# Attention masks on VectorE instead of TensorE, and forgetting rows as a full 128-row matmul

## The chip, the cores and the metric

The kernel runs on one core of one Trainium2 chip. The metric is the device time of one execution in microseconds (us). Before the change the median of three runs is 1434.82 us (1432.43 to 1436.96). The engines are named as in the profile: PE (TensorE, matmuls; PEld its weight loads), DVE (VectorE), ACT (ScalarE), POOL (GpSimd) and SP (SyncE, which issues most of the loads).

## The reference, cut to what matters

256 tokens of 1024 features go through four layers. Three of them have softmax attention that the change touches: layer 0 (16 heads of forgetting attention and 16 of dilated attention) and the two mixers of the second block (8 heads each, with two attentions per head over the same queries).

```python
def forgetting_attention(q, k, v, log_f):
    c = jnp.cumsum(log_f, axis=1).transpose(0, 2, 1)
    ...
        s = jnp.einsum('bqhd,bkhd->bhqk', q[:, q0:e], k[:, :e]).astype(f32) * scale
        s = s + c[:, :, q0:e, None] - c[:, :, None, :e]
        causal = jnp.arange(e)[None, :] <= (q0 + jnp.arange(BLOCK))[:, None]
        p = jax.nn.softmax(jnp.where(causal, s, NEG), axis=-1)

def dilated_pattern(q, k, v, window, dilation):
    ...
    s = jnp.where(mask, s, NEG)
    lse = jax.nn.logsumexp(s, axis=-1)
    p = jnp.exp(s - lse[..., None])
```

The three dilated patterns are merged with weights from their log-denominators. On 256 tokens that equals one softmax over scores to which the logarithm of the number of patterns that hold a key is added, and the kernel computes it so: its dilated mask holds such logarithms, and -1e30 where no pattern holds the key.

## The kernel before

Every product with weights is computed as three matmuls (`mm3`, L177 to L179) on operands that are split into a high and a low part. ScalarE writes the high half of a loaded weight tile (L56), VectorE the low one (L58); this goes on through the whole kernel, a few tiles ahead of use. The weights are used in units; a unit of 128x256 matmuls has 48 of them in two chunks.

Attention runs beside the units, as side work in stages (class `Side`). One attention step treats two heads and both query tiles of 128 tokens. Stage 1 computes the scores on PE: S1 (second query tile, 256 keys for each of two heads, 512 columns; L419) and S0 (first tile, 128 keys, 256 columns; L422), three matmuls each, and adds the mask by more matmuls into the same bank. Stage 2 (`softmax`) runs on VectorE and ScalarE. Stage 3 transposes the probabilities on PE (L456, L458), stage 4 multiplies them with the values (L468, L470). Between the stages stand chunks of weight matmuls: in layer 0 a stage follows after two chunks, in the mixers after one. So what a stage needs from the other engines has the time of one or two chunks to come about.

How a mask gets into the scores before:
- dilated steps (8, first half of layer 0): the identity times the mask, in two parts, four matmuls (`dil`, L557 with 512 columns and L559 with 256)
- forgetting steps (8, second half of layer 0): a matmul of two rows deep, ones times the high and the low part of the accumulated gates (`fox`, L569 and L571), and then the causal mask as identity times mask, 256 columns (`causal`, L429), once for S1 and once for S0
- mixer steps (8 in each of two mixers): the two causal matmuls alone

`softmax` then takes the maxima of S1 and S0 from PSUM on VectorE (L435, L436), ScalarE computes four exponentials from PSUM with these as bias (L441), VectorE the reciprocals (L443; in the mixers times gates, L446) and the scaling of P1 (L448), ScalarE the scaling of P0 (L449).

The tile framework orders the instructions of each engine when the program is built; each engine then works through its own queue in that order, and waits by semaphores.

Of the kernel before, what the change touches and what calls it, by code (L numbers as in the profile page):

```python
# [24 lines left out]
class Weights:  # L25
    """The weights in the order of their use: loaded and split into two float32r parts ahead of it."""
# [48 lines left out]
class Side:  # L75
    """Work in stages that goes between the weight units. A stage that yields "pre" has its next one before a unit."""
# [39 lines left out]
class Stack:  # L116
# [41 lines left out]
    def split_shifts(self):  # L158
        """The shifts of the norms, [(part, chunk), 128 features] in three bfloat16 parts that add up to them."""
# [21 lines left out]
    def evac(self):  # L181
        """What is left to do with the products of the units before; some of it a unit later."""
# [8 lines left out]
    def feature_unit(self, done, chunks=2):  # L191
        """[features, tokens] of a unit's columns."""
# [10 lines left out]
    def token_units(self, *dones):  # L203
        """[tokens, features] of the columns of some units, tile by tile of the tokens."""
# [15 lines left out]
    def finish(self, ahead=True):  # L220
        """The norm of the second tile of tokens."""
# [59 lines left out]
    def rsqrt(self, mul, eps, *var):  # L281
        """1 / sqrt(var * mul + eps) of each, by Newton's steps from a guess on the bits; the guess is negative."""
# [27 lines left out]
    def squares(self, tt, acc):  # L310
        """The sums of the squares of a tile of x, by halves of the features; acc has its banks for the squares."""
# [5 lines left out]
    def rms(self, g, accs, between=0):  # L317
        """xT gets the parts of the normalised tiles of x; g has the scales of the features."""
# [13 lines left out]
    def layer_norm(self, tt, g, b, bT=None, acc=None, rms=None):  # L332
        """Of ALPHA * x + acc; or of the normalised x by the scales in rms, with their norm's factor in this one's."""
# [41 lines left out]
    def transpose(self, tt, src, dr, shift=None, scale=None):  # L375
        """The two parts of src * r * scale + shift go to xT; dr has the scales r of the tokens on its diagonal."""
# [25 lines left out]
    def split_into(self, hi, lo, src, scale=1.0):  # L402
        """The two float32r parts of src * scale; scale is a power of two."""
# [12 lines left out]
    def scores(self, q, kz, extra):  # L416
        S1, S0 = self.bank([128, 2, 256]), self.bank([128, 2, 128])
        for i, (a, b) in enumerate(((0, 0), (0, 1), (1, 0))):
            self.nc.tensor.matmul(S1[:], q[a][:, 128:256], kz[b][:], start=i == 0, stop=False, skip_group_check=True)  # L419
        extra(S1, S0, 1)  # L420
        for i, (a, b) in enumerate(((0, 0), (0, 1), (1, 0))):
            self.nc.tensor.matmul(S0[:], q[a][:, 0:128], kz[b][:, :, 0:128], start=i == 0, stop=False,  # L422
                                  skip_group_check=True)
        extra(S1, S0, 0)
        return S1, S0

    def causal(self, S1, S0, i):
        m = self.cm[:, None, :].to_broadcast([128, 2, 128])
        self.nc.tensor.matmul((S1[:, :, 128:256] if i else S0[:]), self.identr[:], m, start=False, stop=True,  # L429
                              skip_group_check=True)  # L430
# [1002 lines left out]
```

## Time and profile before

| what | value |
|---|---|
| median of three runs | 1434.82 us |
| span of the profiled execution | 1432.7 us |
| PE busy | 1393.4 us (97%), 10075 matmuls |
| PEld busy | 1289.3 us (90%) |
| DVE busy | 1097.8 us (77%), 1816 instructions |
| ACT busy | 828.4 us (58%), 1388 instructions |
| POOL busy | 99.5 us (7%) |
| mean granted TensorE clock | 0.989 |

A busy share is a mean over stages that have different limits. Matmuls overlap: one is listed with 0.28 us where the next starts 0.12 us later, so for PE the distance of the starts tells the cost, and not the duration. The rows below are taken from single stretches for that reason. Layer 0's attention steps lie between 42 and 270 us, the mixers' between 552 and 622 and between 880 and 950 us.

### The profile page before, as it was taken

Reading aid. Unit: us, or ns where it says so; the run is one execution under the profiler, and the core shown is the slowest. Engines: PE = TensorE matmul, PEld = TensorE weight load, DVE = VectorE, ACT = ScalarE, POOL = GpSimd, SP = SyncE. Lnnn points to the kernel's source line nnn. Section 1 sums busy time; section 2 is a strip of 40 time slices with the busy share of each in tenths; the row PEclk is TensorE's granted clock in tenths of the full one; section 3 lists DMA queues with packets and bytes.
Section 4 is the critical chain, followed back from the end, with each engine's and each line's share of the span. In section 5 each row is a group of like instructions: output and inputs, shape, how many; then the busy total and the mean of one; then the engine's idle time right before and its main releaser. Section 6 shows DMA issues by size and latency. Waiting matters only on the chain. (4 is left out here: it accounts for less than half of the span.)

```text
span 1432.7 us, 25068 instructions
## 1 busy us (share of the span) xinstructions
PE 1393.4 (97%) x10075; PEld 1289.3 (90%) x10075; DVE 1097.8 (77%) x1816; ACT 828.4 (58%) x1388; POOL 99.5 (7%) x136
## 2 busy tenths in 40 slices
PE   7999999999999999999999999998999999999995
PEld 7999999789999789989999889987999999999983
DVE  7766656567777679878655388777989989989987
ACT  7665555454455347544444247645777777777762
POOL 1000000000000100010000000003010110120110
PEclk9999999999999999999999999998999999999997
DMA  7633343336444466326455446322989889889882
GB/s 292 233 147 138 129 148 138 134 138 226 155 175 155 132 232 224 118 67 264 178 184 199 176 145 253 118 98 83 361 332 339 314 327 346 307 335 355 309 329 85
DMA packets 45435, 301.50 MB, mean 210 GB/s; under 512 B 6000, under 2 KB 6368, under 8 KB 10624
## 3 DMA queue, kind: packets, MB, share of 16 engines
q1 hardware_dynamic: 42336, 293.40, 55.4%
q0 software_dynamic: 2832, 6.42, 1.7%
q8 instruction: 81, 1.33, 0.4%
q14 instruction: 42, 0.34, 0.1%
q10 hardware_dynamic: 144, 0.01, 0.0%
HBM read 298.73 MB, written 1.05 MB: 209 GB/s over the span
## 5 line engine op out<-in xcount | busy, mean ns | idle before, releaser
L58 DVE TENSOR_TENSOR w_lo<-w_raw,w_hi 128x1024 fp32r<-128x1024 f32 x553 | 673.5, 1249 | 170.0 <-ACT w_hi L56 169.7
L56 ACT ACTIVATE w_hi<-w_raw 128x1024 fp32r<-128x1024 f32 x553 | 560.9, 1056 | 212.2 <-PE ps L179 103.4
L177 PE MATMUL ps<-xT,w_hi 128*128 128x256 f32 x1096 | 310.6, 283 | 0.0
L178 PE MATMUL ps<-xT,w_hi 128*128 128x256 f32 x1096 | 308.0, 281 | 0.0
L179 PE MATMUL ps<-xT,w_lo 128*128 128x256 f32 x1096 | 307.8, 281 | 0.0
L177 PEld LDWEIGHTS ps<-xT,w_hi 128*128 128x128 f32 x1096 | 206.4, 188 | 1.7 <-issue 1.5
L178 PEld LDWEIGHTS ps<-xT,w_hi 128*128 128x128 f32 x1096 | 206.6, 188 | 0.0
L179 PEld LDWEIGHTS ps<-xT,w_lo 128*128 128x128 f32 x1096 | 206.5, 188 | 0.0
L178 PE MATMUL ps<-w_lo,xe 128*128 128x256 f32 x704 | 199.3, 283 | 1.3 <-DVE w_lo L58 1.1
L177 PE MATMUL ps<-w_hi,xe 128*128 128x256 f32 x704 | 198.9, 283 | 0.0
L179 PE MATMUL ps<-w_hi,xe 128*128 128x256 f32 x704 | 198.8, 282 | 0.0
L177 PE MATMUL ps<-w_hi,xT 128*128 128x256 f32 x528 | 148.7, 282 | 0.0
L178 PE MATMUL ps<-w_lo,xT 128*128 128x256 f32 x528 | 147.8, 280 | 0.0
L179 PE MATMUL ps<-w_hi,xT 128*128 128x256 f32 x528 | 146.9, 280 | 0.1
L178 PEld LDWEIGHTS ps<-w_lo,xe 128*128 128x128 f32 x704 | 132.5, 188 | 3.0 <-DVE w_lo L58 2.2
L177 PEld LDWEIGHTS ps<-w_hi,xe 128*128 128x128 f32 x704 | 132.9, 189 | 0.6
L179 PEld LDWEIGHTS ps<-w_hi,xe 128*128 128x128 f32 x704 | 132.6, 188 | 0.0
L177 PEld LDWEIGHTS ps<-w_hi,xT 128*128 128x128 f32 x528 | 100.0, 189 | 0.3
L178 PEld LDWEIGHTS ps<-w_lo,xT 128*128 128x128 f32 x528 | 100.0, 189 | 0.3
L179 PEld LDWEIGHTS ps<-w_hi,xT 128*128 128x128 f32 x528 | 99.2, 189 | 0.4 <-DVE xT L398 0.3
L441 ACT ACTIVATE P<-ps,sm_mx 128x128 f32<-128x128 f32 (+1 forms) x128 | 52.1, 419 | 37.3 <-DVE sm_mx L435 37.3
L1214 POOL TENSOR_TENSOR x<-x,part 128x512 f32<-128x512 f32 x28 | 47.5, 1724 | 337.2 <-ACT part L1210 274.8
(365 smaller groups left out, 2219.9 us busy)
## 6 DMA issues: line engine op xcount, KB each, us to landing
w_raw<-in_wts SPq DMA_DIRECT2D x271, 1024.0 KB, 4.9
w_raw<-in_wth SPq DMA_DIRECT2D x11, 512.0 KB, 4.5
w_raw<-in_ln_g POOLq DMA_DIRECT2D x3, 512.0 KB, 4.2
w_raw<-in_ln_b POOLq DMA_DIRECT2D x3, 512.0 KB, 5.1
x<-in_x SPq DMA_DIRECT2D x4, 256.0 KB, 3.5
out<-x SPq DMA_DIRECT2D x4, 256.0 KB, 2.1
dec<-in_dec POOLq DMA_DIRECT2D x1, 512.0 KB, 9.7
w_raw<-in_final_norm POOLq DMA_DIRECT2D x1, 512.0 KB, 3.8
```

Source lines behind the costliest of these rows:

```text
L56: self.nc.scalar.activation(hi[:, d], t[:, d], AF.Copy)
L58: self.nc.vector.tensor_sub(lo[:, d], t[:, d], hi[:, d].bitcast(F32))
L177: t.matmul(out, l[0], r[0], start=start, stop=False, skip_group_check=True)
L178: t.matmul(out, l[0], r[1], start=False, stop=False, skip_group_check=True)
L179: t.matmul(out, l[1], r[0], start=False, stop=stop, skip_group_check=True)
L441: s.activation(p[:, h, :], src[:, h, :], AF.Exp, bias=mx[:, o + h:o + h + 1], accum_out=rs[:, o + h:o + h + 1])
L1214: nc.gpsimd.tensor_add(x, x, t[:])
```

## The change

PE no longer adds masks. `scores` has three score matmuls per bank, and a fourth in the forgetting steps, for the accumulated gates; that one now has 128 rows, all ones on one side, and on the other two rows of gates and 126 of zeros (two fixed buffers `crs`, cleared once at the start, of which the loads write the first two rows). In `softmax` a combined VectorE operation takes each head's scores from PSUM, adds the mask from SBUF, multiplies by -1, writes the result to the tile of the probabilities and reduces it to its minimum; the exponentials read that tile and write over it. The masks are loaded as plain float32 tiles through GpSimd's queue (before: one load through SyncE's), and four VectorE copies, one ScalarE copy and the split of the dilated mask at the start are gone. Docstrings and comments are gone too, so the line numbers differ.

```diff
-    def scores(self, q, kz, extra):
+    def scores(self, q, kz, row=None):
         S1, S0 = self.bank([128, 2, 256]), self.bank([128, 2, 128])
-        for i, (a, b) in enumerate(((0, 0), (0, 1), (1, 0))):
-            self.nc.tensor.matmul(S1[:], q[a][:, 128:256], kz[b][:], start=i == 0, stop=False, skip_group_check=True)
-        extra(S1, S0, 1)
...
+        for S_, t, n in ((S1, 1, 256), (S0, 0, 128)):
+            ms = [(q[a][:, t * 128:(t + 1) * 128], kz[b][:, :, 0:n]) for a, b in ((0, 0), (0, 1), (1, 0))]
+            if row is not None:
+                ms.append((self.ones[:], row[:, :, 0:n]))
+            for i, (l, r) in enumerate(ms):
+                self.nc.tensor.matmul(S_[:], l, r, start=i == 0, stop=i == len(ms) - 1, skip_group_check=True)
...
-        v.reduce_max(mx[:, 0:2], S1[:], axis=AX, negate=True)
-        v.reduce_max(mx[:, 2:4], S0[:], axis=AX, negate=True)
...
-        for p, src, o in ((P1, S1, 0), (P0, S0, 2)):
+        both = ((P1, S1, mask, 0), (P0, S0, mask[:, 128:256], 2))
+        for p, src, m, o in both:
             for h in range(2):
-                s.activation(p[:, h, :], src[:, h, :], AF.Exp, bias=mx[:, o + h:o + h + 1],
+                v.tensor_tensor_reduce(p[:, h, :], src[:, h, :], m, -1.0, 3e38, ALU.add, ALU.min,
+                                       mx[:, o + h:o + h + 1])
+        for p, src, m, o in both:
+            for h in range(2):
+                s.activation(p[:, h, :], p[:, h, :], AF.Exp, bias=mx[:, o + h:o + h + 1], scale=-1.0,
                              accum_out=rs[:, o + h:o + h + 1])
...
-        nc.sync.dma_start(dm[:], a["dm"])
+        self.causal = c.tile([128, 256], F32, name="causal")
+        nc.gpsimd.dma_start(self.causal[:], a["dm"][:, 256:512])
...
-            ones = big.tile([2, 128], F32R, name="ones2")
-            dm = [big.tile([128, 256], F32R, name=f"dm{i}") for i in range(2)]
+            self.ones = big.tile([128, 128], F32R, name="ones")
+            crs = [big.tile([128, 2, S], F32R, name=f"cr{i}") for i in range(2)]
+            nc.gpsimd.memset(self.ones[:].bitcast(F32), 1.0)
+            for t in crs:
+                nc.gpsimd.memset(t[:].bitcast(F32), 0.0)
...
+            dilated = big.tile([128, 256], F32, name="dilated")
+            nc.gpsimd.dma_start(dilated[:], a["dm"][:, 0:256])
...
-                    nc.vector.tensor_copy(self.identr[:], self.ident)
-                    nc.vector.tensor_copy(self.cm[:], dmf[:, 256:384])
-                    nc.vector.tensor_scalar(ones[:], self.ident[0:2, :], 0.0, 1.0, op0=ALU.mult, op1=ALU.add)
-                    self.split_into(dm[0][:], dm[1][:], dmf[:, 0:256])
                     self.split_shifts()
...
-                cr = io.tile([2, 2, S], F32R, name="cr")
+                cr = crs[p % 2]
                 for j in range(2):
                     nc.gpsimd.dma_start(cr[j:j + 1], cc[j][2 * p:2 * p + 2, :])
```

The order of the instructions on an engine, as the programs are built, at two places. First PE's queue in the first forgetting step before (`ps` are the scores, `kz` the keys, `q` the queries, `cr` the gates, `cm` the causal mask, `w_hi` the next unit's weights):

```order
L419 MATMUL ps<-kz_86,q_1853 128x512
L419 MATMUL ps<-kz_87,q_1853 128x512
L419 MATMUL ps<-kz_86,q_1854 128x512
L569 MATMUL ps<-cr,ones_81 128x512
L429 MATMUL ps<-cm,identr 128x2x128
L422 MATMUL ps<-kz_86,q_1853 128x256
L422 MATMUL ps<-kz_87,q_1853 128x256
L422 MATMUL ps<-kz_86,q_1854 128x256
L571 MATMUL ps<-cr,ones_81 128x256
L429 MATMUL ps<-cm,identr 128x256
L177 MATMUL ps<-w_hi,xT_126 128x256
```

And the same step's rows on PE in the changed kernel, where all score matmuls stand on one line:

```order
L424 MATMUL ps<-kz_89,q_1835 128x512
L424 MATMUL ps<-kz_90,q_1835 128x512
L424 MATMUL ps<-kz_89,q_1836 128x512
L424 MATMUL ps<-cr_82,ones 128x512
L424 MATMUL ps<-kz_89,q_1835 128x256
L424 MATMUL ps<-kz_90,q_1835 128x256
L424 MATMUL ps<-kz_89,q_1836 128x256
L424 MATMUL ps<-cr_82,ones 128x256
L177 MATMUL ps<-w_hi,xT_129 128x256
```

The two causal matmuls are gone, and the gates' matmul closes each bank. Second, VectorE's queue in the first mixer, from the hidden layer of the compression (`hid`) over the first step's softmax to its scaling of P1, before:

```order
L885 TENSOR_TENSOR hid_5666<-ps,b_5652 32x256
L435 TENSOR_REDUCE sm_mx<-ps 128x2
L436 TENSOR_REDUCE sm_mx<-ps 128x2
L58 TENSOR_TENSOR w_lo<-w_raw,w_hi 128x1024 x2
L443 RECIPROCAL sm_rs<-sm_rs 128x4
L58 TENSOR_TENSOR w_lo<-w_raw,w_hi 128x1024
L446 TENSOR_TENSOR sm_rs<-sm_rs,gt 128x2 x2
L58 TENSOR_TENSOR w_lo<-w_raw,w_hi 128x1024
L448 TENSOR_SCALAR P_6174<-P_6174,sm_rs 128x256 x2
```

And VectorE at the same place in the changed kernel, down to the same reciprocal:

```order
L867 TENSOR_TENSOR hid_5640<-ps,b_5626 32x256
L436 ISA P_6144,sm_mx<-ps,causal 128x256
L436 ISA sm_mx 128x1
L436 ISA P_6144,sm_mx<-ps,causal 128x256
L436 ISA sm_mx 128x1
L436 ISA P_6145,sm_mx<-ps,causal 128x128
L436 ISA sm_mx 128x1
L436 ISA P_6145,sm_mx<-ps,causal 128x128
L436 ISA sm_mx 128x1
L58 TENSOR_TENSOR w_lo<-w_raw,w_hi 128x1024 x2
L442 RECIPROCAL sm_rs<-sm_rs 128x4
```

Eight instructions stand where two stood; what follows them is in the same order as before.

## Rows read from the trace of the kernel before

**Rows 1.** Busy us (instructions) of PE, PEld, DVE, ACT, POOL; PE clock, DMA share, GB/s.

```profile
42.00:270.00 228.00, 227.47 (x1747) 208.69 (x1747) 145.69 (x241) 134.02 (x310) 8.03 (x16) 1.00 0.41 149
551.00:569.00 18.00, 16.94 (x135) 15.72 (x134) 17.61 (x32) 12.85 (x31) 0.00 (x0) 1.00 0.72 267
```

**Rows 2.** PE by time, first forgetting step: start us, us, engine, line, tiles.

```profile
160.71 0.86 PE L419 MATMUL ps<-kz,q 128*128 128x512 f32 x3
161.51 0.49 PE L569 MATMUL ps<-cr,ones 2*128 2x512 f32 x1
161.93 0.39 PE L429 MATMUL ps<-cm,identr 128*128 128x256 f32 x1
162.15 0.52 PE L422 MATMUL ps<-kz,q 128*128 128x256 f32 x3
162.60 0.38 PE L571 MATMUL ps<-cr,ones 2*128 2x256 f32 x1
162.91 0.39 PE L429 MATMUL ps<-cm,identr 128*128 128x256 f32 x1
163.13 0.28 PE L177 MATMUL ps<-w_hi,xT 128*128 128x256 f32 x1
```

**Rows 3.** PE by time, mask matmuls of a dilated step.

```profile
102.60 0.63 PE L557 MATMUL ps<-dm,identr 128*128 128x512 f32 x2
103.06 0.52 PE L422 MATMUL ps<-kz,q 128*128 128x256 f32 x3
```

**Rows 4.** PE by time, a causal matmul of a mixer step.

```profile
570.19 0.28 PE L429 MATMUL ps<-cm,identr 128*128 128x256 f32 x1
570.30 0.52 PE L422 MATMUL ps<-kzs,q 128*128 128x256 f32 x3
```

**Rows 5.** PE by time, a 24-row matmul behind a 512-column one.

```profile
623.76 0.40 PE L179 MATMUL ps<-w_hi,yc 128*128 128x512 f32 x1
624.09 0.60 PE L382 MATMUL ps<-chunk,shifts 24*128 24x512 bf16 x2
```

**Rows 6.** VectorE's groups by form: count, busy us, mean ns, idle before.

```profile
L435 DVE TENSOR_REDUCE sm_mx<-ps 128x2 f32<-128x512 f32 x32 | 21.8, 681 | 3.2 <-PE ps L429 2.0
L436 DVE TENSOR_REDUCE sm_mx<-ps 128x2 f32<-128x256 f32 x32 | 13.4, 418 | 1.4 <-PE ps L429 1.1
L611 DVE SCALAR_TENSOR_TENSOR y<-o,g 128x256 f32<-128x256 f32 x16 | 6.6, 413 | 0.4 <-PE o L470 0.4
L1164 DVE SCALAR_TENSOR_TENSOR he<-th,ps 128x128 f32<-128x128 f32 x8 | 2.3, 282 | 0.1
L446 DVE TENSOR_TENSOR sm_rs<-sm_rs,gt 128x2 f32<-128x2 f32 x32 | 3.6, 154 | 0.3
```

**Rows 7.** By time: scalings of probabilities, and transposes on PE that follow them.

```profile
50.58 0.41 PE L458 MATMUL ps<-cst,P 128*128 128x128 f32 x2 [0.48 <-DVE P L448]
...
559.41 0.62 PE L456 MATMUL ps<-cst,P 128*128 128x128 f32 x2 [0.69 <-ACT P L449]
560.40 0.41 PE L458 MATMUL ps<-cst,P 128*128 128x128 f32 x2 [0.37 <-DVE P L448]
...
568.22 0.69 ACT L449 ACTIVATE P<-P,sm_rs 128x128 f32<-128x128 f32 x2 [2.19 <-DVE sm_rs L446]
568.84 0.27 PE L456 MATMUL ps<-cst,P 128*128 128x128 f32 x1
...
575.06 0.62 DVE L448 TENSOR_SCALAR P<-P,sm_rs 128x256 f32<-128x256 f32 x2
575.81 0.27 PE L456 MATMUL ps<-cst,P 128*128 128x128 f32 x1
```

**Rows 8.** By time, a dilated step: last scaling, and first transpose.

```profile
106.02 0.70 ACT L449 ACTIVATE P<-P,sm_rs 128x128 f32<-128x128 f32 x2 [0.25 <-DVE sm_rs L443]
109.28 0.27 PE L456 MATMUL ps<-cst,P 128*128 128x128 f32 x1
```

**Rows 9.** ScalarE by time: its first split of a weight.

```profile
10.24 2.00 ACT L56 ACTIVATE w_hi<-w_raw 128x1024 fp32r<-128x1024 f32 x2 [2.89 <-DMA w_raw<-in_wts]
```

More of the change, by code (lines that the diff above doesn't have):

```diff
@@ L427, in causal @@
[L427 to L430, printed above, removed]
-    def softmax(self, P, S1, S0, gate=None):
+        for S_, t, n in ((S1, 1, 256), (S0, 0, 128)):
[4 more added lines that the diff above has]
+                self.nc.tensor.matmul(S_[:], l, r, start=i == 0, stop=i == len(ms) - 1, skip_group_check=True)
@@ L433, in softmax @@
+        return S1, S0
+    def softmax(self, P, S1, S0, mask, gate=None):
         v, s = self.nc.vector, self.nc.scalar
         mx, rs = self.small(4, "sm_mx"), self.small(4, "sm_rs")
-        v.reduce_max(mx[:, 0:2], S1[:], axis=AX, negate=True)
-        v.reduce_max(mx[:, 2:4], S0[:], axis=AX, negate=True)
         P1 = P.tile([128, 2, 256], F32, name="P1")
         P0 = P.tile([128, 2, 128], F32, name="P0")
-        for p, src, o in ((P1, S1, 0), (P0, S0, 2)):
+        both = ((P1, S1, mask, 0), (P0, S0, mask[:, 128:256], 2))
+        for p, src, m, o in both:
@@ L492, in setup @@
         self.pick = cst[:, 200:210]
-        self.identr, self.cm = (c.tile([128, 128], F32R, name=n) for n in ("identr", "cm"))
         self.xT = [c.tile([128, 8, S], F32R, name=f"xT{i}") for i in range(2)]
@@ L519, in even, with shifts @@
             P = ctx.enter_context(tc.tile_pool(name="l0p", bufs=2))
-            dmf = io.tile([128, 384], F32, name="v")
-            self.setup(dmf)
-            def masks():
+            dilated = big.tile([128, 256], F32, name="dilated")
+            nc.gpsimd.dma_start(dilated[:], a["dm"][:, 0:256])
+            self.setup()
+            def shifts():
                 yield
@@ L526, in masks @@
                 with self.W.behind(self.W.after), self.W.behind(self.W.after_act):
-                    nc.vector.tensor_copy(self.identr[:], self.ident)
-                    nc.vector.tensor_copy(self.cm[:], dmf[:, 256:384])
-                    nc.vector.tensor_scalar(ones[:], self.ident[0:2, :], 0.0, 1.0, op0=ALU.mult, op1=ALU.add)
-                    self.split_into(dm[0][:], dm[1][:], dmf[:, 0:256])
                     self.split_shifts()
-            self.pend.append(masks())
+            self.pend.append(shifts())
             def fa_done(ps):
@@ L551, in fa_done @@
                 self.split_into(cc[0][:], cc[1][:], z)
-            def dil(S1, S0, i):
-                for j in range(2):
-                    m = dm[j][:, None, :].to_broadcast([128, 2, 256])
-                    if i:
-                        nc.tensor.matmul(S1[:], self.identr[:], m, start=False, stop=j == 1, skip_group_check=True)
-                    else:
-                        nc.tensor.matmul(S0[:], self.identr[:], m[:, :, 128:256], start=False, stop=j == 1,
-                                         skip_group_check=True)
             def fox(p):
-                cr = io.tile([2, 2, S], F32R, name="cr")
+                cr = crs[p % 2]
                 for j in range(2):
                     nc.gpsimd.dma_start(cr[j:j + 1], cc[j][2 * p:2 * p + 2, :])
-                def f(S1, S0, i):
-                    if i:
-                        nc.tensor.matmul(S1[:], ones[:], cr[:], start=False, stop=False, skip_group_check=True)
-                    else:
-                        nc.tensor.matmul(S0[:], ones[:], cr[:, :, 0:128], start=False, stop=False,
-                                         skip_group_check=True)
-                    self.causal(S1, S0, i)
-                return f
+                return cr
             pairs, vs, gs = {}, {}, {}
@@ L600, in attend @@
                 q, kz = pairs.pop(i)
-                S1, S0 = self.scores(q, kz, fox(i) if ch < 8 else dil)
+                S1, S0 = self.scores(q, kz, fox(i) if ch < 8 else None)
                 yield "pre"
-                P1, P0 = self.softmax(P, S1, S0)
+                P1, P0 = self.softmax(P, S1, S0, self.causal if ch < 8 else dilated)
                 yield
@@ L799, in attend @@
                 gate = [gt[:, tt, c0:c0 + 8].rearrange("p (g h) -> p g h", g=2)[:, :, p] for tt in range(2)]
-                S1, S0 = self.scores([t[:, p, :] for t in q], kz[kind], self.causal)
+                S1, S0 = self.scores([t[:, p, :] for t in q], kz[kind])
                 yield "pre"
-                P1, P0 = self.softmax(P, S1, S0, gate)
+                P1, P0 = self.softmax(P, S1, S0, self.causal, gate)
                 yield
@@ L1363, in constants @@
     n = sum(((d >= 0) & (d <= wd) & (d % r == 0)).astype(np.int64) for wd, r in ((128, 1), (512, 4), (2048, 16)))
-    c["dm"] = np.concatenate([np.where(n > 0, np.log(np.maximum(n, 1)), NEG), np.where(s <= t, 0.0, NEG)],
+    c["dm"] = np.concatenate([np.where(n > 0, np.log(np.maximum(n, 1)), NEG), np.zeros((128, 128)),
+                              np.where(s <= t, 0.0, NEG)],
                              axis=1).astype(np.float32)
```

6 lines of the change are left out of this document (1 added, 5 removed).

## The prediction

> **What bounds the kernel now.** I read the busy time by stretch first, then the PE instructions in order of time around the three kinds of attention step, then VectorE's groups by form, then what stands beside the few waits of PE. In the stretch that holds the first layer's sixteen attention steps PE is busy 227.47 of 228.00 us at full granted clock while VectorE is busy 145.69 and ScalarE 134.02 [rows 1]. There the matmul stream is the bound: an instruction taken out of it takes its step (the time from its start to the next one's start) out of the run, as long as nothing that PE later needs comes later than PE gets to it. The exception is a stretch at the head of each mixer: between 551 and 569 us VectorE is busy 17.61 of 18.00 us and PE only 16.94 [rows 1]. There VectorE is the bound, and whatever is added to it is paid. The change takes from PE and gives to VectorE, so these two stretches decide.
>
> **PE, forgetting steps (8).** In [rows 2] three 512-column score matmuls start at 160.71; the matmul with the forgetting rows (L569, 2 rows deep) starts 0.80 later, the next one 0.42 after that, and the unit's next weight matmul (L177) comes at 163.13. The step takes 2.42 us. A 512-column matmul on 128 rows has a step of 0.23 us (two in 0.46) [rows 3], a 256-column one 0.11 to 0.12 [rows 4]; I use 0.23 and 0.115. With these alone the ten matmuls would take 4 x 0.23 + 6 x 0.115 = 1.61 us, so about 0.8 us of each step is the price of going in and out of the 2-row form twice: L419 to L569 0.80 instead of 0.69, L569 to L429 0.42 instead of 0.23, L429 to L422 0.22 instead of 0.115, and again around L571. A 24-row matmul elsewhere shows the way in too: 0.33 us from a 512-column matmul to L382 [rows 5] where 0.23 is the step between equals. After the change the step has four 512- and four 256-column matmuls, all on 128 rows: 1.38 us. Saved: 2.42 - 1.38 = 1.04 us, times 8 = 8.3 us; 1.8 of it are the two causal matmuls, 6.5 the 2-row form.
>
> The Trainium skill, page "TensorE: Matmul & The Clock Gate", section "LDWEIGHTS (loading the stationary operand)", says that the load time depends on the columns and not on the contraction rows, so that a 32x128 load costs what a 128x128 load does. By it full rows save nothing, and only the two causal matmuls would count. The load alone is not what the rows above show as the price, so I go by them, and keep the other outcome as the first rival.
>
> **PE, dilated steps (8) and mixer steps (16).** A dilated step drops two 512- and two 256-column mask matmuls: 2 x 0.23 + 2 x 0.115 = 0.69 us, times 8 = 5.5. A mixer step drops two 256-column ones: 0.23 us, times 16 = 3.7. Sum taken out of PE: 8.3 + 5.5 + 3.7 = 17.5 us.
>
> **VectorE and ScalarE.** A softmax had two maxima, 681 and 418 ns [rows 6]. It now has four operations that read scores from PSUM and a mask from SBUF and write the masked scores, each followed by a one-column instruction that brings out the minimum. The nearest rows for the wide ones are L611 (PSUM and SBUF in, SBUF out, 256 columns, 413 ns) and L1164 (128 columns, 282 ns); for the narrow one L446 (154 ns) [rows 6]. Full price: 2 x 413 + 2 x 282 + 4 x 154 = 2006 ns against 1099, so +0.9 us. Low end: the narrow ones hide, and neighbours overlap, as two operations of L448 take 0.62 us together [rows 7]; then +0.13. I take x = 0.6 us a softmax, above the middle since each narrow one must wait for the wide one in front of it. ScalarE's four exponentials stay, now from SBUF and in place; the first may start after one 256-column operation instead of after the 512-column maximum, so on an idle VectorE the chain to the probabilities is about as long as before.
>
> **Where x is covered.** In the first layer the probabilities lie ready long before PE transposes them: the last scaling ends at 106.02 + 0.70 = 106.72 and the transposes start at 109.28 [rows 8], 2.6 us of slack; the other steps but one have 2.0 to 4.0. If that cover were gone, each step would cost x. The exception is the first step, where PE already waits 0.48 us for VectorE (the row at 50.58) [rows 7]. There the chain hangs on VectorE's queue and not on the scores, so the 0.69 us that PE saves ahead of it is lost, and some of x: I take 1.0 us. First layer: 8.3 + 5.5 - 1.0 = 12.8 us.
>
> **Where x is paid.** In each mixer PE waits for the probabilities of the first step (0.69 us for ScalarE, then 0.37 more for VectorE), takes up the second step's as they are made (its scaling runs 568.22 to 568.91, PE starts at 568.84) and the third's with 0.13 us to spare (575.68 and 575.81) [rows 7]. Behind the maxima in VectorE's queue stand the low halves of the weights (L58) and then the scalings that PE waits for, so each of these three is later by x, and PE's own saving ahead of it (0.23, 0.23, some 0.14) is only waited away: 3x + 0.6 us a mixer. The other five have more spare or an idle VectorE ahead of them. Both mixers, since the second repeats the first: 3.7 - 2 x (3 x 0.6 + 0.6) = -1.1 us, a small loss; with x = 0.13 it is +1.7, with 0.9 it is -2.9.
>
> **The start.** The 192 KB of masks leave SyncE's queue, where they stood behind the first weight, and 256 KB go by GpSimd's queue, behind its memsets, of which there are three more, and ahead of the six small loads of norm shifts, needed only after some 23 us. ScalarE waits 2.89 us for the first weight [rows 9]; 256 KB at the 267 GB/s of [rows 1] is 1.0 us if all of it cuts in ahead of that weight, and 0 if it lands behind. I take 0.2. The first mask is not read before some 45 us, and the four VectorE copies that disappear save nothing in a stretch where PE streams. GpSimd's loads of the forgetting rows keep their two buffers.
>
> **Sum.** 12.8 - 1.1 - 0.2 = 11.5 us. The profiled span is 1432.7 us; the median of the runs shown is 1434.8, 2.1 us above it, which I leave as it is: 1434.8 - 11.5 = 1423.3 us. Ends: 12.8 + 1.7 = 14.5 us saved (1420.3) and 12.8 - 2.9 - 1.0 = 8.9 (1425.9).
>
> **The rivals.** First, the depth of the forgetting matmul is not what costs, but, say, the matmuls' own place in the group: then 6.5 us stay and the time is 1423.3 + 6.5 = 1429.8. The rule of the Trainium skill named above would give this outcome. For it: the 2-row weight load itself is no different. Against it: every 2-row and 24-row neighbour in [rows 2] and [rows 5] shows the longer step. Second, PE's saving comes through whole, because VectorE's queue is put together so that nothing ahead of the scalings is later: 1434.8 - 17.5 = 1417.3. For it: at the end of a stage VectorE has idle time. Against it: the 17.61 of 18.00. Third, slower: the new wide operation is of a kind that no row of this trace shows (the built program has it as an instruction of its own class), and it may run well below one column a cycle. The price is paid in the mixers' first three steps, 6x in all, and from x = 2 also in the first layer, whose shortest slack that is. The saving is gone when 6x = 12.6 + 3.7 - 1.2 = 15.1, at x = 2.5; with x = 3.0 the mixers lose 15.5 and, with slacks of 2.0 to 2.6 overrun in four steps, the first layer about 2, which gives 1434.8 - 12.6 + 15.5 + 2 = 1439.7. Against it: VectorE's other two-input rows lie within 20 ns of each other whatever they compute. That the change doesn't do what it says is excluded: the order above has the mask matmuls gone from PE.
>
> **How the numbers follow.** Forecast, with its ends 1420.3 to 1425.9: 0.77. PE's saving whole, 1417.3: 0.08. The depth costs nothing, 1429.8: 0.06. The new operation slow: 0.09, of it 0.05 slower and 0.04 within what can be told apart. A measurement of this kernel can tell about 0.3% (4.3 us) from no change, so the line is at 1430.5. Faster: 0.77 + 0.08 + 0.03 (half of the first rival, which stands almost on the line) = 0.88; same 0.03 + 0.04 = 0.07; slower 0.05. The range reaches from the whole saving to the first rival: 1417 to 1429.
>
> **What would show it.** Right: a forgetting step of 1.4 us from its first score matmul to the next unit's L177, a dilated one without its 0.69; PE busy some 17 us less in all; softmaxes with 1.6 to 1.8 us of VectorE time; PE's waits for the transposed probabilities grown from 1 us to about 3 in each mixer. Wrong: a step of 0.42 still standing behind the matmul with the forgetting rows; wide operations over 0.6 us; PE idle ahead of transposes in the first layer's later steps; a first weight that lands later than 10.2 us.

## The result, and the profile after

The changed kernel takes 1419.52 us (median of four runs, 1418.13 to 1420.65) against 1435.29 us for the kernel before on the same chip (1432.43 to 1436.96): a ratio of 0.9889, 95% interval 0.9877 to 0.9901. It is faster by 15.8 us, where 11.5 were forecast. The profiled execution has a span of 1417.2 us, against 1432.7 before.

To see where the time went, I took each weight matmul (L177 to L179; both programs have 8652 of them, in the same order) and subtracted its start before from its start after. The changes of that difference, stretch by stretch:

| stretch (times of before) | what it holds | difference, us |
|---|---|---|
| 0 to 42 | start | +0.2 |
| 42 to 101 | first four dilated steps | -3.4 |
| 101 to 160 | last four dilated steps | -2.8 |
| 160 to 278 | eight forgetting steps | -8.3 |
| 278 to 500 | no attention | 0.0 |
| 500 to 523 | no attention | -1.3 |
| 523 to 551 | no attention | -0.2 |
| 551 to 622 | first mixer | +0.2 |
| 622 to 860 | no attention | 0.0 |
| 860 to 950 | second mixer | 0.0 |
| 950 to the end | experts and the rest | +0.2 |

So the first layer's attention gives 14.5 us, the mixers nothing, and 1.3 us stand where the change has no instruction.

The page of the changed kernel, busy us (share of the span) and instructions of each engine:

```profile
PE 1373.6 (97%) x9995; PEld 1276.7 (90%) x9995; DVE 1102.9 (78%) x2004; ACT 834.4 (59%) x1387; POOL 102.6 (7%) x141
```

PE has lost 19.8 us of busy time (some 17 were forecast) and 80 matmuls. Now the forgetting step on PE, by time, in the changed kernel (start us, us, engine, line, tiles; this answers [rows 2]):

```profile
154.71 0.86 PE L424 MATMUL ps<-kz,q 128*128 128x512 f32 x3
155.40 0.39 PE L424 MATMUL ps<-cr,ones 128*128 128x512 f32 x1
155.63 0.52 PE L424 MATMUL ps<-kz,q 128*128 128x256 f32 x3
155.99 0.28 PE L424 MATMUL ps<-cr,ones 128*128 128x256 f32 x1
156.10 0.28 PE L177 MATMUL ps<-w_hi,xT 128*128 128x256 f32 x1
```

From the first score matmul to the next unit's L177 it is 156.10 - 154.71 = 1.39 us, where [rows 2] had 2.42. The gates' matmul stands among the others at their own distances, 0.23 and 0.11.

The softmax on VectorE, groups by form of the changed kernel (count, busy us, mean ns, idle before; this answers [rows 6]):

```profile
L436 DVE CUSTOM_DVE_ANT_0 P<-ps,causal 128x256 f32<-128x256 f32 x48 | 18.3, 411 | 0.1
L436 DVE CUSTOM_DVE_ANT_0 P<-ps,causal 128x128 f32<-128x128 f32 x48 | 12.0, 282 | 0.1
L436 DVE DVE_READ_ACCUMULATOR2_ANT sm_mx<- 128x1 f32 x128 | 10.1, 79 | 0.0
L436 DVE CUSTOM_DVE_ANT_0 P<-ps,dilated 128x256 f32<-128x256 f32 x16 | 6.0, 411 | 0.0
L436 DVE CUSTOM_DVE_ANT_0 P<-ps,dilated 128x128 f32<-128x128 f32 x16 | 4.0, 287 | 0.1
```

In all 50.4 us for 32 softmaxes, 1.58 us each, against (21.8 + 13.4) / 32 = 1.10 before: x is 0.48 us. The wide operations cost what L611 and L1164 of [rows 6] cost, 411 and 282 to 287 ns; the one-column reads take 79 ns, half of the row that had been put in for them.

What PE waited for, over the whole run (the changed kernel: us, times, longest):

```profile
PE ps L455 <- ACT P L448: 5.0, 4, 1.3
PE ps L457 <- DVE P L447: 0.9, 3, 0.4
```

These are the transposes' waits for probabilities; before, the same two came to 1.4 and 1.2 us. In the first mixer they stand at its first two steps, and the third step does not wait (the changed kernel by time; the last bracket is the wait):

```profile
543.84 0.62 PE L455 MATMUL ps<-cst,P 128*128 128x128 f32 x2 [1.14 <-ACT P L448]
...
544.84 0.41 PE L457 MATMUL ps<-cst,P 128*128 128x128 f32 x2 [0.38 <-DVE P L447]
...
554.52 0.33 PE L455 MATMUL ps<-cst,P 128*128 128x128 f32 x1 [1.32 <-ACT P L448]
```

Together 2.84 us, against 0.69 + 0.37 = 1.06 in [rows 7]. The two stretches of [rows 1], at the same work in the changed kernel (columns as there):

```profile
42.00:266.00 224.00, 223.80 (x1755) 209.60 (x1754) 150.73 (x342) 139.20 (x315) 8.09 (x16) 1.00 0.44 158
...
535.26:553.26 18.00, 16.43 (x129) 15.01 (x127) 17.91 (x44) 12.96 (x30) 0.00 (x0) 1.00 0.71 266
```

In layer 0 PE is still busy throughout. At the head of the mixer VectorE is busy 17.91 of 18.00 us, and PE, with less to do, only 16.43.

The 1.3 us between 500 and 523 are TensorE's clock. Two windows of the kernel before, and then the same work in the changed kernel (columns as in [rows 1]; the third number from the end is the granted clock):

```profile
515.00:523.40 8.40, 6.30 (x38) 5.67 (x38) 6.83 (x19) 1.19 (x2) 0.00 (x0) 0.80 0.42 146
520.00:523.40 3.40, 3.40 (x18) 3.40 (x17) 3.40 (x5) 0.95 (x2) 0.00 (x0) 0.50 0.37 130
```

```profile
500.00:508.40 8.40, 6.29 (x51) 5.66 (x51) 6.83 (x21) 1.77 (x3) 0.00 (x0) 1.00 0.41 146
```

Before, 3.4 us ran at a granted clock of 0.50 (1.2 of 2.4 GHz), after 5.0 us in which PE had been busy for 2.9. After, with the same pattern of waits, no such fall: 51 matmuls in the window instead of 38. In a second profile of the same changed kernel it is there again, with a mean clock of 0.83 over 10 us:

```profile
500.00:510.00 10.00, 7.91 (x52) 7.28 (x51) 7.70 (x23) 3.52 (x8) 0.00 (x0) 0.83 0.47 179
```

A third profile has it too. So this gain belongs to the profile and not to the change.

### The profile page after: what moved, and what is told of

Same layout as the page of the kernel before. It is cut to its first block, busy times and chain, and to the rows that moved or that the text cites. A ratio compares the mean times of both kernels' runs of the same rounds, so it can differ in the third digit from the quotient of the medians.

```text
span 1417.2 us, 25109 instructions
## 1 busy us (share of the span) xinstructions
PE 1373.6 (97%) x9995; PEld 1276.7 (90%) x9995; DVE 1102.9 (78%) x2004; ACT 834.4 (59%) x1387; POOL 102.6 (7%) x141
## 3 DMA queue, kind: packets, MB, share of 16 engines
HBM read 298.79 MB, written 1.05 MB: 212 GB/s over the span
## 5 line engine op out<-in xcount | busy, mean ns | idle before, releaser
L56 ACT ACTIVATE w_hi<-w_raw 128x1024 fp32r<-128x1024 f32 x553 | 560.9, 1056 | 214.6 <-PE ps L179 100.7
L177 PE MATMUL ps<-xT,w_hi 128*128 128x256 f32 x1096 | 310.9, 284 | 0.0
L179 PE MATMUL ps<-xT,w_lo 128*128 128x256 f32 x1096 | 308.0, 281 | 0.0
L177 PEld LDWEIGHTS ps<-xT,w_hi 128*128 128x128 f32 x1096 | 206.8, 189 | 1.7 <-issue 1.5
L179 PEld LDWEIGHTS ps<-xT,w_lo 128*128 128x128 f32 x1096 | 206.8, 189 | 0.0
L177 PE MATMUL ps<-w_hi,xe 128*128 128x256 f32 x704 | 199.1, 283 | 0.0
L179 PE MATMUL ps<-w_hi,xe 128*128 128x256 f32 x704 | 199.0, 283 | 0.0
L177 PE MATMUL ps<-w_hi,xT 128*128 128x256 f32 x528 | 148.0, 281 | 0.0
L179 PE MATMUL ps<-w_hi,xT 128*128 128x256 f32 x528 | 146.6, 280 | 0.0
L177 PEld LDWEIGHTS ps<-w_hi,xe 128*128 128x128 f32 x704 | 133.1, 189 | 0.6
L179 PEld LDWEIGHTS ps<-w_hi,xe 128*128 128x128 f32 x704 | 132.9, 189 | 0.0
L177 PEld LDWEIGHTS ps<-w_hi,xT 128*128 128x128 f32 x528 | 99.4, 188 | 0.3
L179 PEld LDWEIGHTS ps<-w_hi,xT 128*128 128x128 f32 x528 | 98.9, 188 | 0.1
L440 ACT ACTIVATE P<-P,sm_mx 128x128 f32<-128x128 f32 (+1 forms) x128 | 57.0, 446 | 28.8 <-DVE sm_mx L436 28.5
```

Source lines behind the costliest of these rows:

```text
L56: self.nc.scalar.activation(hi[:, d], t[:, d], AF.Copy)
L177: t.matmul(out, l[0], r[0], start=start, stop=False, skip_group_check=True)
L179: t.matmul(out, l[1], r[0], start=False, stop=stop, skip_group_check=True)
L440: s.activation(p[:, h, :], p[:, h, :], AF.Exp, bias=mx[:, o + h:o + h + 1], scale=-1.0, accum_out=rs[:, o + h:o + h + 1])
```

## The experiments

The theory: (a) a matmul of another depth among 128-row ones is paid in going in and out of its form, and that is 6.5 us of the eight forgetting steps; (b) PE's mask matmuls count in full in layer 0, where VectorE's extra time is covered; (c) in the mixers the masks gain nothing, because VectorE's extra time is paid at the head. Rivals: the depth itself, or the gates matmul's place; and that the first layer's gain comes from something that went with the masks. Each diff is against the changed kernel unless the text says otherwise. Stretches are named by the times of before, as in the table above, and what a stretch gives is counted against before.

**Two rows again.** The gates' matmul takes two rows of the same buffers.

```diff
-                ms.append((self.ones[:], row[:, :, 0:n]))
+                ms.append((self.ones[0:2, :], row[0:2, :, 0:n]))
```

> The changed kernel with the forgetting matmuls two rows deep again (the same two rows of the same tiles); masks stay on VectorE. If going in and out of the 2-row form is what costs, each of the 8 forgetting steps is 0.8 us longer on PE than in the changed kernel (2.2 us from its first score matmul to the next unit, against 1.4), all else equal: 1419.5 + 6.5 = 1426.0 us. If the depth does not cost, 1419.5 us and steps of 1.4 us.

Measured: 1428.54 us (four runs, ratio to before 0.9948, 0.9929 to 0.9967). The stretch of the forgetting steps gives 1.9 us against before, where the change gives 8.3: the form costs 6.4 us, 0.80 a step. The step by time:

```profile
155.58 0.87 PE L424 MATMUL ps<-kz,q 128*128 128x512 f32 x3
156.38 0.49 PE L424 MATMUL ps<-cr,ones 2*128 2x512 f32 x1
156.80 0.62 PE L424 MATMUL ps<-kz,q 128*128 128x256 f32 x3
157.35 0.38 PE L424 MATMUL ps<-cr,ones 2*128 2x256 f32 x1
157.66 0.39 PE L177 MATMUL ps<-w_hi,xT 128*128 128x256 f32 x1
```

157.66 - 155.58 = 2.08 us instead of 1.39, and the matmul behind that L177 comes 0.22 us later where it came 0.12 later: together 0.80. Of the 9 us in the medians the rest lies outside these steps: this profile's start is 1.1 us later, and it has more of the low clock.

**Full rows alone.** The kernel before with the full gates matmul. The VectorE copy that made the two rows of ones at the start is gone with it; GpSimd clears and fills the new buffers.

```diff
-            ones = big.tile([2, 128], F32R, name="ones2")
+            ones = big.tile([128, 128], F32R, name="ones")
+            crs = [big.tile([128, 2, S], F32R, name=f"cr{i}") for i in range(2)]
...
-                cr = io.tile([2, 2, S], F32R, name="cr")
+                cr = crs[p % 2]
```

> The kernel before with nothing but the forgetting rows as a full 128-row matmul; masks stay matmuls. If the 2-row form costs 0.8 us a step: 1435.3 - 6.5 = 1428.8 us, with forgetting steps of 1.6 us (2.42 before). If the depth does not cost: 1435.3 us. Of the whole gain of 15.8 us the masks would then hold the rest, 9.3 or 15.8.

Measured: 1426.92 us (four runs, ratio 0.9935, 0.9918 to 0.9953). The forgetting stretch gives 6.2 us (its first step takes 1.64 us), the last four dilated steps 0.0, and the first four 0.9: there one of the four start copies is missing. With the run above: 6.2 to 6.4 for the form and 1.9 to 2.1 for the causal matmuls make the change's 8.3.

**Two rows, side by side.** The same two 2-row matmuls, but the one closes the first bank and the other opens the second.

```diff
-                ms.append((self.ones[:], row[:, :, 0:n]))
+                ms.insert(3 * t, (self.ones[0:2, :], row[0:2, :, 0:n]))
```

> As the run with two rows, but in the first query tile the 2-row matmul comes first in its bank, so that the step's two 2-row matmuls stand next to each other. If the change of form is what costs, there is one way in and one way out where there were two, so half of the 0.8 us: steps of 1.8 us, 1422.8 us. If each 2-row matmul costs its 0.4 us wherever it stands: steps of 2.2 us, 1426.0 us.

Measured: 1425.59 us (one run). The forgetting stretch gives 5.1 us, so what is left of the price is 3.2 us, 0.40 a step: half, with as many 2-row matmuls as before. By time:

```profile
156.67 0.87 PE L424 MATMUL ps<-kz,q 128*128 128x512 f32 x3
157.46 0.61 PE L424 MATMUL ps<-cr,ones 2*128 2x512 f32 x2
158.00 0.63 PE L424 MATMUL ps<-kz,q 128*128 128x256 f32 x3
158.47 0.28 PE L177 MATMUL ps<-w_hi,xT 128*128 128x256 f32 x1
```

From 156.67 to 158.47 it is 1.80 us. There is one way in and out instead of two. What is paid is the change of form and not the shallow matmul.

**64 rows.** Half the depth instead of a sixty-fourth.

```diff
-                ms.append((self.ones[:], row[:, :, 0:n]))
+                ms.append((self.ones[0:64, :], row[0:64, :, 0:n]))
```

> The changed kernel with the forgetting matmuls 64 rows deep. If any depth but the full 128 rows is another form: forgetting steps of 2.2 us, layer 0 longer by 6.4 us, 1426 us. If the price is that of few rows, it falls with the depth: 64 rows cost half or less, 1422.5 us or under.

Measured: 1429.92 us (one run); the forgetting stretch gives 2.0 us, as with two rows. The step by time:

```profile
155.28 0.87 PE L424 MATMUL ps<-kz,q 128*128 128x512 f32 x3
156.08 0.49 PE L424 MATMUL ps<-cr,ones 64*128 64x512 f32 x1
156.50 0.61 PE L424 MATMUL ps<-kz,q 128*128 128x256 f32 x3
157.04 0.38 PE L424 MATMUL ps<-cr,ones 64*128 64x256 f32 x1
157.35 0.38 PE L177 MATMUL ps<-w_hi,xT 128*128 128x256 f32 x1
```

2.07 us, the same as with two rows within 0.01. The price is the same at 2 and at 64 rows; depths between 64 and 128 were not tried.

**The mixers as before.** The changed kernel with causal matmuls and `reduce_max` in the mixers alone.

```diff
+            if pe:
+                m = self.cm[:, None, :].to_broadcast([128, 2, 128])
+                self.nc.tensor.matmul(S_[:, :, n - 128:n], self.identr[:], m, start=False, stop=True, skip_group_check=True)
...
+        if pe:
+            v.reduce_max(mx[:, 0:2], S1[:], axis=AX, negate=True)
+            v.reduce_max(mx[:, 2:4], S0[:], axis=AX, negate=True)
...
-                S1, S0 = self.scores([t[:, p, :] for t in q], kz[kind])
+                S1, S0 = self.scores([t[:, p, :] for t in q], kz[kind], pe=True)
...
-                P1, P0 = self.softmax(P, S1, S0, self.causal, gate)
+                P1, P0 = self.softmax(P, S1, S0, None, gate)
```

> The changed kernel, but the two mixers as before: causal masks by matmuls, maxima from PSUM. Layer 0 stays as changed. The mixers were 0.2 us longer after the change than before, though PE lost 1.8 us of matmuls in each. If that is because VectorE gives back what PE saves, undoing it there changes nothing: 1419.5 us within 1, mixers within 0.3 us of both kernels. If something else lengthened them (a shifted load, say) and the masks on VectorE do save there, it gets slower by up to 3.7 us: 1423.

Measured: 1421.94 us (four runs, ratio 0.9915, 0.9897 to 0.9933). Against before the mixers stand at 0.0 and +0.1 us, in the changed kernel at +0.2 and 0.0. The head of the first mixer, same columns as above:

```profile
535.40:553.40 18.00, 16.95 (x135) 15.72 (x134) 17.61 (x32) 12.84 (x31) 0.00 (x0) 1.00 0.69 264
```

On the same chip the change itself took 1421.53 us in a later comparison (below). Two of the four start copies are back in this kernel, since the causal matmuls need them. VectorE is back at the 17.61 of [rows 1]. Taking the masks off PE in the mixers neither costs nor gives anything that can be measured: 1.8 us of PE's work per mixer are exchanged for 1.8 us of waiting (2.84 - 1.06).

**The reduction twice.** Each combined operation is issued twice.

```diff
-                v.tensor_tensor_reduce(p[:, h, :], src[:, h, :], m, -1.0, 3e38, ALU.add, ALU.min,
-                                       mx[:, o + h:o + h + 1])
+                for _ in range(2):
+                    v.tensor_tensor_reduce(p[:, h, :], src[:, h, :], m, -1.0, 3e38, ALU.add, ALU.min,
+                                           mx[:, o + h:o + h + 1])
```

> The changed kernel with each masked minimum computed twice in a row, so 1.2 us more of VectorE per softmax (32 of them). If layer 0 covers VectorE's part by slack (2 to 3 us between the last scaling and the transposes) and the mixers' first three steps pay it: layer 0 within 2 us of the changed kernel's, each mixer 3 x 1.2 = 3.6 us longer, 1419.5 + 7.2 + 1.5 = 1428 us. If VectorE has room in the mixers too: 1420 us. If the chain's length counts in every step: 32 x 1.2 = 38 us, 1458 us.

Measured: 1444.32 us (one run). In layer 0 twice the VectorE time costs 1.1 us over sixteen steps: the cover is real, but used up, for in eight of the steps ScalarE's last scaling now ends 0.1 to 0.2 us after the first transpose has started, where in the change it ends 1.0 to 3.5 us ahead of it in all but the first step. In the mixers it costs 12.7 and 10.9 us, several times what I expected. PE's waits, and the longest of them in the first mixer:

```profile
PE ps L456 <- ACT P L449: 17.6, 7, 4.1
```

```profile
614.03 0.33 PE L456 MATMUL ps<-cst,P 128*128 128x128 f32 x1 [4.08 <-ACT P L449]
```

The waits for ScalarE's scaling rise from 5.0 to 17.6 us in seven places, and longer waits are followed by falls of the clock: the trace has four stretches at 0.5 in the mixers, 6.8, 3.4, 3.4 and 3.4 us, where the change has none. 12.6 us of waiting and, at half speed, up to 8.5 us of clock are 21 of the 23.6 us; the rest is not accounted for.

But this is not the changed kernel with a larger x alone: its instructions are also in another order. The longest wait, 4.08 us, stands at the last step of each mixer. There PE goes from the scores to the transposes with no weight matmul between, where the kernel before and the change have 24 of them. So 8.2 of the 17.6 us come with an order that has lost its cover. At each mixer's first two steps the waits grow by 2.1 us, from 2.84 to 4.90, where 3 x 1.58 = 4.7 would follow from the prediction's formula. Where the cover of the mixers ends between x = 0.48 and x = 0.48 + 1.58 = 2.06 is open.

**The start's copies again.** Four VectorE copies and one ScalarE copy, as before at the start, into tiles that nothing reads.

```diff
+                    nc.vector.tensor_copy(idle[0][:], self.ident)
+                    nc.vector.tensor_copy(idle[1][:], self.causal[:, 128:256])
+                    nc.vector.tensor_scalar(idle[0][0:2, :], self.ident[0:2, :], 0.0, 1.0, op0=ALU.mult, op1=ALU.add)
+                    self.split_into(idle[2][:], idle[2][:], dilated[:])
                     self.split_shifts()
```

> The changed kernel with the four VectorE copies and the ScalarE copy of the masks put back at the start, into tiles that nobody reads. If the first dilated step was not late after the change because these copies had stood ahead of it in a full VectorE queue, its softmax starts 0.6 to 0.9 us later than in the changed kernel and PE waits that much longer at its transposes: 1420.2 us. If the copies do not matter, the first step is as in the changed kernel: 1419.5 us.

Measured: 1426.04 us (one run). The stretch from 42 to 101 gives 1.7 us instead of 3.4; the later steps of layer 0 are as in the change. First exponential and first transpose of the first step by time, of the changed kernel and then of this one:

```profile
45.92 0.51 ACT L440 ACTIVATE P<-P,sm_mx 128x256 f32<-128x256 f32 x1
...
49.06 0.27 PE L455 MATMUL ps<-cst,P 128*128 128x128 f32 x1
```

```profile
48.53 0.51 ACT L440 ACTIVATE P<-P,sm_mx 128x256 f32<-128x256 f32 x1
...
52.31 0.33 PE L455 MATMUL ps<-cst,P 128*128 128x128 f32 x1 [1.63 <-ACT P L448]
```

Counted from the step's first score matmul (42.37, here 43.56, before 42.15), the first exponential starts 3.56 us later in the change, 4.97 later here and 4.98 before: the copies hold this chain back by 1.4 us. With them PE waits 1.63 us at the first step; without them it does not wait for ScalarE at all. Part of the 1.63 has another source: here ScalarE splits a weight (L56, 1.05 us from 50.92 on) ahead of the scaling that PE waits for, and neither the kernel before nor the change has a split at that place. How copies of 0.7 us in all move the chain by 1.4 is not shown; the run with full rows alone, which lacks only the shortest of them, has its first exponential at 3.73. The other 4.8 us of the single time lie outside: a start 1.2 us later and more of the low clock (40.7 against 28.2 us in the two profiles).

**Values as wide matmuls.** If a change of form costs, the products with the values (64 columns) should gain from zeros in the other half.

```diff
-            r = slice(h * 64, (h + 1) * 64)
-            self.nc.tensor.matmul(o[r, 0:256], v0[:, h, :], PT[:, h, 0:2, :], start=start, stop=False,
+            r = slice(h * 64, h * 64 + 128)
+            self.nc.tensor.matmul(o[:, 0:256], v0[:, r], PT[:, h, 0:2, :], start=start and h == 0, stop=False,
```

> The changed kernel with the products with the values (64 columns of weights per head before, two heads side by side) as matmuls with 128 columns, the other head's 64 being zeros: four full matmuls that add into one output. Before, PE pays a change of form into and out of the 64-column matmuls; a step's four pairs cost about 1.0 us of PE, the way in and out and the slower step behind them included. With full columns a 256-column float32 matmul steps by 0.22 us and a 128-column one by 0.11 us, 0.65 us in all. If the change of form is the price as it is for the rows: 32 x 0.35 = 11 us less, 1408 us. If running both heads side by side is worth more than the change of form costs: 1419.5 us or slower.

Measured: 1432.11 us (nine runs, ratio to before 0.9981, 0.9968 to 0.9995): slower than the change, by 5.2 us in layer 0's steps. In the mixers two more tiles had to share buffers to make room for the zeros (not shown above), so they are not read here. A step's products by time, in the changed kernel and then in this one:

```profile
92.19 0.66 PE L467 MATMUL o<-PT,v 128*64 128x256 f32 x4
92.67 0.40 PE L469 MATMUL o<-PT,v 128*64 128x128 f32 x4
93.00 0.39 PE L177 MATMUL ps<-xT,w_hi 128*128 128x256 f32 x1
```

```profile
93.19 0.59 PE L467 MATMUL o<-PT,vz 128*128 128x256 f32 x2
93.62 0.38 PE L469 MATMUL o<-PT,vz 128*128 128x128 f32 x2
93.84 0.60 PE L467 MATMUL o<-PT,vz 128*128 128x256 f32 x2
94.27 0.38 PE L469 MATMUL o<-PT,vz 128*128 128x128 f32 x2
94.41 0.37 PE L177 MATMUL ps<-xT,w_hi 128*128 128x256 f32 x1
```

1.22 us instead of 0.81. My expectation had overlooked what the counts say: one product is two matmuls (x2), and with 64 columns those of the two heads start within 14 ns of each other, four in the time of two, while with 128 columns the second head's come after the first's.

**Fewer forms.** The value products of two steps stand behind one another, and the 24-row shift matmuls (L382, [rows 5]) get 128 rows.

```diff
-                o = self.o.tile([128, S], F32, name="o")
...
-                self.pv(o, PT, vt[:, 0], vt[:, 1], True, True)
+                waiting.append((PT, ch))
+                if len(waiting) < 2:
+                    return
+                o = self.o.tile([128, 2, S], F32, name="o")
+                for n, (PT, c) in enumerate(waiting):
...
+                    self.pv(o[:, n], PT, vt[:, 0], vt[:, 1], True, True)
...
-        r = slice(64 * (i // 2), 64 * (i // 2) + 24)
-        return self.shifts[r, i % 2], self.chunk[r]
+        return self.shifts[:, i % 2], self.chunk[:, i // 2]
```

> The changed kernel with fewer changes of form on PE: the 64-column products with the values of two steps (in the mixers, of the two attentions over one output) stand next to each other, and the shift matmuls of the norms have 128 rows instead of 24, the others zeros. If each way into and out of another form costs 0.3 us (0.09 in, 0.09 out, 0.1 at the second matmul behind), 16 places in the attention steps and 8 at the norms give 24 x 0.3 = 7 us: 1412.5 us. If holding back a step's product costs elsewhere what that saves: 1419.5 us.

Measured: 1417.49 us (four runs, ratio 0.9876, 0.986 to 0.9891). The change on the same chip, word for word:

> The changed kernel once more, beside the others of this call: 1419.5 us, within 2.

Measured: 1421.53 us (six runs, ratio 0.9901, 0.9886 to 0.9915). The intervals overlap. By the traces layer 0 gains 2.0 us over the change, but the second mixer loses 2.4. At its last step VectorE's queue has the conversion of a table (`before`) ahead of the softmax, and waits there for the table's load; PE then waits for the probabilities:

```profile
927.25 0.29 DVE L1034 CAST before<-beforef 128x256 bf16<-128x256 f32 x1 [2.24 <-DMA beforef<-in_before]
...
930.81 0.33 PE L454 MATMUL ps<-cst,P 128*128 128x128 f32 x1 [2.05 <-ACT P L447]
```

The weight matmuls between this step's scores and its transposes are the 24 that the change has there too. The first mixer has the same pairs and no such table, and loses 0.3 us.

**Fewer forms, mixers left alone.** The same without the pairs in the mixers, and the change once more beside it on one chip.

> The change, with the value products of two steps side by side in layer 0 and the shift rows as 128-row matmuls (as in e8), but the mixers' value products step by step as in the change. If e8 gave 2.4 us back in the second mixer only because there the last step's transposes stood right behind its softmax with no weights between, and the rest of e8 was a saving of matmul forms: 2.0 us less than the change in layer 0 and 1.0 less between the mixers, in all about 3.0 us under the run of the change on the same chip, and both mixers as in the change within 0.3. If the lower median of e8 was only the spread of the clock's low stretches: within 1 us of the change's median.

> The change once more, word for word, so that e10 has it on the same chip: 1419.5 to 1421.5 us, ratio to before 0.989 to 0.990.

Measured: 1416.89 us (1416.01 to 1417.9, ratio 0.987, 0.9855 to 0.9885) and, for the change, 1422.22 us (ratio 0.9904, 0.9888 to 0.9919). The intervals do not meet: this version beats both kernels. Its second mixer has the conversion of the table behind the softmax's masked minima again, and PE does not wait at the last step. The reason for the loss that the expectation gives, no weights between the softmax and the transposes, does not hold. A pair's products by time:

```profile
90.77 0.66 PE L466 MATMUL o<-PT,v 128*64 128x256 f32 x4
91.25 0.40 PE L468 MATMUL o<-PT,v 128*64 128x128 f32 x4
91.47 0.65 PE L466 MATMUL o<-PT,v 128*64 128x256 f32 x4
91.90 0.44 PE L468 MATMUL o<-PT,v 128*64 128x128 f32 x4
92.27 0.38 PE L176 MATMUL ps<-xT,w_hi 128*128 128x256 f32 x1
```

1.50 us for two steps where the change has 2 x 0.81, and one slow first weight matmul (0.22 us from L176 to the next) instead of two. Layer 0 gives 16.2 us against before, the change 14.5 to 14.8 in its three profiles: 1.4 to 1.7 us, a little under the 2.0 expected. Between the mixers it is 1.0 us more, as expected. That is 2.4 to 2.7 of the 5.3 us between the medians. In the two profiles the start (1.5 us) and fewer low-clock stretches behind 950 us (2.0 us) speak for this version as well, and one more such stretch in its second mixer against it (1.5 us); the edit touches none of these, and whether the remaining 2.6 to 2.9 us of the medians are more than chance is not settled.

## Why the prediction was right, point by point

**The number.** 1419.52 us lies in the stated range but 0.8 us below the forecast's own ends (1420.3 to 1425.9); the two later medians of the same kernel, 1421.53 and 1422.22, lie within them. Of the 4.3 us by which the saving was larger than forecast, the profile puts 1.7 in the first layer, 0.9 in the mixers and 1.3 in the clock, which differs between executions; the rest is the distance between the profiles' 15.4 us and the medians' 15.8. The first two errors point the same way, so the sum did not come out by one cancelling the other.

**Forgetting steps: right to the hundredth.** 1.04 us a step was forecast from [rows 2] and [rows 3], 8.30 / 8 = 1.04 was measured. That the form's change is the price, and not the depth, was argued from neighbours before; the runs with 2 rows, 64 rows and two side by side show it.

**Dilated steps: right.** 0.71 us a step (2.84 over the last four), 0.69 forecast.

**The first rival fell, but not its rule.** The Trainium skill's page "TensorE: Matmul & The Clock Gate", section "LDWEIGHTS (loading the stationary operand)", has the load's time depend on columns alone. The equal steps at 2 and 64 rows (2.08 and 2.07 us) fit a price that doesn't grow with depth. What the rule leaves out is the price of leaving and regaining the 128-row form, 0.40 us each time here, and on this the trace decides: the rival's 1429.8 us did not come.

**The first step: wrong.** I took 1.0 us as lost there, since the chain hung on VectorE's queue. But the change also takes copies out of that very queue, and I had said that they "save nothing in a stretch where PE streams". Without them the stretch from 42 to 101 gave 3.4 us, 0.5 more than four mask savings of 0.71; with them put back it gave 1.7, which is 1.2 less. That is near the 1.0 that I took, but a weight split ahead of ScalarE's scaling is in it, so how near is partly chance. Layer 0: 14.5 us where 12.8 were forecast, 1.5 of the difference from this step and the rest from the 0.02 us by which each dilated step gave more.

**x: mis-sized, and two steps pay instead of three.** 0.6 us was taken, between ends of 0.13 and 0.9, and 0.48 measured: the accumulator's read is a 79 ns instruction and not the 154 ns of its nearest row, and the wide operations overlap a little (40.3 us busy in all, where 64 x 411 and 64 x 284 ns are 44.5). Put into the prediction's own formula, 2 x (3 x 0.48 + 0.6) = 4.1 us of cost against 3.7 of saving gives -0.4 where -1.1 was forecast; the profile has -0.2. The waits grew from 1.06 to 2.84 us in the first mixer, "about 3". But the sum has three steps that are later by x each, and the rows show only two that wait; the third, which has been held up with PE behind the second, does not. That VectorE's extra time is paid at the head, up to what PE saved, holds; the count of the steps does not. The second rival (all of PE's saving) needed the mixers to keep theirs: they kept none of it, in the change as in the kernel that put the causal matmuls back.

**The third rival fell.** The combined operation is as fast as L611 and L1164, 411 and 282 ns, far from x = 2.5. The kernel that issued it twice is 9 us above before at x = 2.06, where I had put the point of no gain at 2.5. It does not settle where that point lies, since 8.2 us of its waits come with another order of the instructions.

**The start and the clock.** Forecast 0.2 us later, and 0.2 later in the profile. The other two profiles of the same kernel start 1.9 and 1.1 us later than before, so this term is not known to better than 2 us. The clock's 1.3 us was in no term; the two later profiles of the change have a 3.4 us stretch of low clock there again. In those two comparisons the change gained 14.3 and 13.7 us, which is about what layer 0 gives (14.8) less part of the later start.

## What to carry to other kernels

Where PE streams, count a shallow or narrow matmul not by its size but by the changes of form around it: fill the rows of a shallow one with zeros, or put two such matmuls side by side. Filling up the columns of narrow ones lost time here. A mask moved from PE to VectorE is worth what PE would have spent only where the probabilities have slack; ask at each stage which engine the stage waits for, and expect nothing where VectorE is already full. When a chain hangs on an engine's queue, list everything that the change takes out of that queue as well as what it puts in, and look at what stands ahead of the chain in the program as built: one softmax behind a table's conversion made PE wait 2 us.

## What the runs showed of the hardware

- Between 128-row matmuls, one with 2 rows or one with 64 costs the same extra 0.40 us, and two of them side by side cost it once.
- Changes of the column count cost too: from 128 to 64 columns the step of the last matmul, of the last narrow one and of the first wide one afterwards are each about 0.1 us longer; joining two such groups saved about 0.2 us.
- Exponentials that read SBUF took longer here than those that read PSUM. ScalarE's groups by form, before and then after:

```profile
L441 ACT ACTIVATE P<-ps,sm_mx 128x256 f32<-128x256 f32 x64 | 29.8, 470 | 37.3 <-DVE sm_mx L435 37.3
```

```profile
L440 ACT ACTIVATE P<-P,sm_mx 128x256 f32<-128x256 f32 x64 | 32.1, 503 | 28.3 <-DVE sm_mx L436 27.9
```

503 instead of 470 ns for 256 columns; the instruction also writes over its input and has another scale, so which of these makes it slower is not shown. In layer 0 PE no longer waits for this chain; in the mixers' first two steps it does, and what the 33 ns are worth there was not measured.

- TensorE's clock falls to 0.50 for 3.4, 6.8 or 17.1 us at much the same places (near 505 and 965 us in the changed kernel), but not in every execution: the three profiles of the change have spans of 1417.2, 1420.5 and 1420.7 us, through this and through the start.
